# Index scores woven in portions into the left-over projections, and the first conv and attention spread over later ones

## The chip, the cores and the metric

The kernel runs on one core of a Trainium2 chip. Times are device microseconds of that core, medians over runs. Its engines are TensorE (PE; its weight loads are PEld), VectorE (DVE), ScalarE (ACT), GpSimd (POOL) and SyncE (SP), which here issues the transfers. Each engine takes its instructions in the order in which the compiled program holds them.

## The reference

A trunk of two layers over 2048 tokens of width 1024, in fp32. The even layer is an attention over 256 selected keys beside a causal depthwise convolution; the odd layer is a short convolution with gates.

```python
# even layer, u = rms_norm(x) @ w_in, split into q, k, v, qi, ki, wi, gate_a, glu_b, gate_b
dots  = einsum('bqhd,bsd->bqhs', qi, ki)                 # index scores, 8 heads of 64
score = einsum('bqh,bqhs->bqs', wi, relu(dots))
score = where(key <= query, score, -inf)
_, sel = top_k(score, 256)
a = softmax(q . k[sel] * 64**-0.5) . v[sel]              # 8 heads
a = a * silu(gate_a)
c = causal_depthwise_conv(g_lin * sigmoid(g_gate), cb_w) + cb_bias      # 31 taps
c = silu(layer_norm(c)) * silu(gate_b)
x = x + concat([a, c]) @ w_out
# odd layer, u = rms_norm(x) @ w_in, split into b_gate, c_gate, xin, gate
y = b_gate * causal_depthwise_conv(c_gate * xin, conv_w)                # 3 taps
x = x + (y * silu(gate)) @ w_out
out = rms_norm(x)
```

## The kernel before

The tokens are worked in 4 chunks of 512, each of 4 blocks of 128. Products of fp32 accuracy are made of three fp16 products (`mm3`, lines L189 to L191: high by high, high by low, low by high). `weight` (L195) loads a tile of weights; at its first use the tile is scaled on ScalarE (L210, L211), split on GpSimd (L212) and written back for later chunks (L213).

**Stage 1** makes everything of the even layer that all chunks need. For each chunk `project` computes keys, values, index queries and index keys. `index` (L720) computes a chunk's index scores: for each block, each stretch of up to 1024 keys and each head TensorE writes a tile `ps_i` (L737), ScalarE takes its Relu (L739), and VectorE adds it to the scores `sc` with the head's weight (L741). `select` (L752) then finds for two blocks at a time the 256th largest score of each row: it guesses a threshold, counts with two Sign passes on ScalarE (L792, `junk`), corrects it on VectorE (L796 to L807), and does so several times; then come the closing operations on VectorE, which count (L817), take the best 16 beyond the threshold (L822, L748 to L750), pick (L830, L831) and write a mask (L835); `bad` (L839) flags rows that were not settled. Chunk 0 has an exact selection instead (`general`, L276). `rest` holds what a chunk's projection leaves over: queries (`queries`, units "q") and the channels of the convolution and the gates (`channels`, units "g"), as a generator whose units the driver draws one by one.

Two more generators run in stage 1. `cn0` is the convolution of chunk 0: 120 multiply-adds of VectorE on the tile `cv` (L243), then its layer norm (L256 to L272) and four stores to `mc_dr`. `att` (`first_attention`, L860) is the attention of chunk 0, 32 heads in 4 blocks: logits on TensorE, mask and maximum on VectorE (L345), exponential (L352) and cast (L354) on ScalarE, a product on GpSimd (L355), a transpose through SP, values on TensorE (L372 to L374); at a block's end L396 to L404 on VectorE, and its store to `ma_dr` (L868).

**Stage 2** goes chunk by chunk. It begins at `mix(0)`: the loads `mh` and `ml` from `mc_dr` (L1141) and from `ma_dr` (L1143). `out_even` (L1013) multiplies the mix by the output weights `in_woe` in 8 tiles of 24 matmuls `ps_w<-mh/ml`, and VectorE adds the residual (L1023). The norm of these (L160 to L171, L1045) feeds the odd layer, whose first matmul is `ps_w<-xh`. Two units of gates, `ps_w<-xh` as well, stand around `out_even`; they store to `ga_dr` (L229). The attention of the later chunks and their convolution (tile `ps_c`, L243) run beside the odd layers.

What sets the order: a scheduler places each instruction by its place in the program and by priority; `weave(main, steps, (generator, rate), ...)` (L129) draws one unit of `main` after another and, with each, so many steps of the fillers as the rate says. While it draws fillers, `state["gate"]` is the last matmul of the main unit, and an instruction given to `paced` (L121) may not be placed ahead of it; this puts no wait on the chip.

Of the kernel before, what the change touches and what calls it, by code (L numbers as in the profile page):

```python
# [21 lines left out]
P = 128  # L22
# [21 lines left out]
NWT = 2  # L44
LOOK = 2
ALONE = 1
ATR = 3.5
CE, CX, CN0, CNR, R0, R1, R2 = 1.5, 3.0, 1.0, 0.85, 1.65, 1.65, 2.3
ORDER = ('ggqgqg', 'ggqgqg', 'gggg', 'qq')
EX = 1  # L50
TQ, TP = 2, 4
NA, NB1, KE, LG = 9, 7, 2, 1

SX = 2.0 ** 5
SW = 2.0 ** 8
# [19 lines left out]
def trunk_kernel(ctx: ExitStack, tc: tile.TileContext, xT, pos, wE, woE, wO, woO, par, tab, outT):  # L75
# [49 lines left out]
    def drain(gen):  # L125
        for _ in gen:
            pass

    def weave(main, steps=99, *fills):  # L129
        owed = [0.0] * len(fills)  # L130
        for n, _ in enumerate(main):
            state["gate"] = state["mm"]
            for i, (gen, rate) in enumerate(fills):
                owed[i] += rate
                while owed[i] >= 1.0:
                    owed[i] -= 1.0
                    next(gen, None)
            state["gate"] = None
            if n + 1 == steps:
                break  # L140
# [286 lines left out]
    with ExitStack() as es:  # L427
# [25 lines left out]
        def stats(c, held=None):  # L453
            eng = V if c <= STV else G
            acc = p0.tile([P, CH], FP32, name="ssum", bufs=1)
            for k in range(KD):
                x = held[k] if held else x_tile(c, k)
                square_into(p0, acc, x, k == 0, eng, (lambda: e1.tile([P, CH], FP32, name="th")) if c <= 1 else None)
            return acc
# [45 lines left out]
        def reload(c):  # L505
            xh = xp.tile([P, KD, CH], F16, name="xh")
            xl = xp.tile([P, KD, CH], F16, name="xl")
            for k in range(0, KD, 4):
                SP.dma_start(out=xh[:, k:k + 4, :], in_=xs_dr[c][:, 0, k:k + 4])
                SP.dma_start(out=xl[:, k:k + 4, :], in_=xs_dr[c][:, 1, k:k + 4])  # L510
            return xh, xl
# [206 lines left out]

        def index(c, qst, blocks):
            scs = {}  # L720
            first = cvp.tile([P, NJ, CH], FP32, name="cv") if c == 0 else None
            for i in blocks:
                b = c * TT + i
                W = (b + 1) * P
                if c == 0:
                    sc = first[:, i, 0:W]
                else:
                    sc = scp.tile([P, W], FP32, name=f"sc{i}", padded_shape=[P, (NB - TT + i + 1) * P])
                sm = tk.tile([P, 2], FP32, name=f"sm{i}")
                for sgi, s0 in enumerate(range(0, W, 1024)):  # L730
                    w = min(1024, W - s0)
                    for h in range(H):
                        ps = ps_i.tile([P, 1024], FP32, name="ps_i")
                        for r0 in range(0, w, 512):
                            r = min(512, w - r0)
                            for a in range(2):
                                T.matmul(out=ps[:, r0:r0 + r], lhsT=qst[:, h, i * P:(i + 1) * P], rhs=ki[:, a, s0 + r0:s0 + r0 + r], start=a == 0, stop=a == 1)  # L737
                        rl = e1.tile([P, 1024], FP32, name="relu")
                        A.activation(out=rl[:, 0:w], in_=ps[:, 0:w], func=AF.Relu)  # L739
                        kw = {"accum_out": sm[:, sgi:sgi + 1]} if h == H - 1 else {}  # L740
                        V.scalar_tensor_tensor(out=sc[:, s0:s0 + w], in0=rl[:, 0:w], scalar=wi[:, b, h:h + 1],  # L741
                                               in1=tiny[:, s0:s0 + w] if h == 0 else sc[:, s0:s0 + w],
                                               op0=ALU.mult, op1=ALU.add, **kw)
                scs[b] = (sc, sm, W)
            return scs

        def best16(out, x):
            V.max(out=out[:, 0:8], in_=x)  # L748
# [184 lines left out]
        def rest(c, xs):  # L933
            qs, ch = queries(c, xs), channels(c, xs)
            for unit in ORDER[c]:
                next(qs if unit == "q" else ch)
                yield
            yield from qs
            yield from ch

        def scan(c, xs):
            qst = project(c, xs)
            select(c, index(c, qst, (0, 1)))
            select(c, index(c, qst, (2, 3)))

        a, b, d = score_slot(3, 4), score_slot(0, 3), score_slot(1, 3)
        held = [a[:, k, :] for k in range(4)] + [b[:, k, :] for k in range(3)] + [d[:, 0, :]]
# [4 lines left out]
        qst = project(0, xs)  # L952
        x1 = first_normalize(1, acc, held)
        select_all(0, index(0, qst, (2, 3)))
        scan(1, x1)
        x2 = normalize(2, stats(2))
        r0 = rest(0, reload(0))
        weave(r0, NA)
        scan(2, x2)
        weave(r0)  # L960
        x3 = normalize(3, stats(3))
        r1 = rest(1, reload(1))

        def conv_out(j, x):
# [3 lines left out]

        cn0 = conv_norm(0, cvp, p0, ps_m, conv_out)
        att = first_attention()  # L970
        weave(r1, NB1, (cn0, CE), (att, ATR))
        scan(3, x3)
        weave(r1, 99, (cn0, CE), (att, ATR))
        state["scanned"] = True
        r2 = rest(2, reload(2))
        weave(r2, 99, (cn0, CE), (att, ATR))
        drain(cn0)
        held_last = reload(3)
        weave(rest(3, held_last), 99, (att, ATR))
        drain(att)  # L980


# [311 lines left out]
```

## Time and profile before

| | |
|---|---|
| median of 3 runs | 2196.25 us (2194.11 to 2197.8) |
| profiled execution | 2196.97 us, span 2195.2 us |
| granted TensorE clock, mean | 0.969 |
| TensorE busy | 1990.9 us (91%), 12252 matmuls |
| VectorE busy | 1663.6 us (76%) |
| ScalarE busy | 1174.1 us (53%) |
| GpSimd busy | 806.0 us (37%) |

Busy times are sums over a whole span with two unlike stages: stage 1 lasts to about 849 us, where the first output matmul starts, and the first odd matmul starts at 928.4 us. The clock is a share of full speed, of 2.4 GHz.

### The profile page before, as it was taken

The page shows a single profiled execution, that of the slowest core. Times are in us where ns is not written, and L with a number is a line of the kernel's source. Part 1 is how long each engine was busy: PE and PEld are TensorE (multiplying, and loading weights), DVE is VectorE, ACT ScalarE, POOL GpSimd, SP SyncE. Part 2 cuts the span into 40 slices and gives each one's busy share as a digit, 9 for nine tenths or more (in the row PEclk, how much of TensorE's full clock was granted, in tenths as well). Part 3 has the DMA queues.
Part 4 walks back from the last instruction along what each step waited for, and adds up shares of the span by engine and source line. Part 5 has one row for each costly group of instructions (what it writes and reads, how often), then busy time and mean ns, then how long its engine had stood idle before and what let it go on. Part 6 is the DMA issues. An engine that isn't in the chain of part 4 may idle for free. (4 is left out here: it accounts for less than half of the span.)

```text
span 2195.2 us, 34791 instructions
## 1 busy us (share of the span) xinstructions
PE 1990.9 (91%) x12252; PEld 1076.5 (49%) x12252; DVE 1663.6 (76%) x3485; ACT 1174.1 (53%) x2407; POOL 806.0 (37%) x761
## 2 busy tenths in 40 slices
PE   5777889898999999699999999999999999999997
PEld 3644464555464543244444454454544554444446
DVE  7999979998989884978875988873888887243224
ACT  5656656566477857367773645563555566121111
POOL 4765344535142412246762533441433454000000
PEclk9889999999999999899999999999999999999999
DMA  6445446334646476569875677785868798423234
GB/s 236 169 158 203 170 167 240 106 118 148 195 120 182 114 240 234 181 205 227 234 184 162 184 205 175 186 187 138 185 153 216 168 191 179 140 99 135 96 108 161
DMA packets 405475, 378.78 MB, mean 173 GB/s; under 512 B 313393, under 2 KB 333617, under 8 KB 384561
## 3 DMA queue, kind: packets, MB, share of 16 engines
q1 hardware_dynamic: 405296, 376.54, 60.5%
q8 instruction: 96, 1.57, 0.3%
q14 instruction: 83, 0.67, 0.1%
HBM read 214.35 MB, written 88.70 MB: 138 GB/s over the span
## 5 line engine op out<-in xcount | busy, mean ns | idle before, releaser
L355 POOL TENSOR_TENSOR pp<-lg,pp 128x512 f16<-128x512 f32 (+3 forms) x320 | 340.4, 1087 | 626.3 <-ACT pp L354 544.0
L189 PE MATMUL ps_w<-xh,wt 128*128 128x512 f16 (+1 forms) x1376 | 513.1, 374 | 7.9 <-DVE x L1023 4.2
L190 PE MATMUL ps_w<-xl,wt 128*128 128x512 f16 (+1 forms) x1376 | 513.7, 373 | 0.0
L191 PE MATMUL ps_w<-xh,wt 128*128 128x512 f16 (+1 forms) x1376 | 513.2, 373 | 0.0
L190 PEld LDWEIGHTS <-wt 128*128 128x128 f16 x2112 | 209.2, 99 | 247.4 <-issue 33.8
L189 PEld LDWEIGHTS <-wt 128*128 128x128 f16 x2112 | 209.7, 99 | 235.8 <-issue 17.7
L191 PEld LDWEIGHTS <-wt 128*128 128x128 f16 x2112 | 209.2, 99 | 234.8 <-issue 13.9
L243 DVE SCALAR_TENSOR_TENSOR ps_c<-cin,cwt,ps_c 128x512 f32<-128x512 f32 x348 | 261.2, 751 | 28.0 <-ACT ps_c L241 23.9
L352 ACT ACTIVATE lg<-lg,m 128x512 f32<-128x512 f32 (+3 forms) x320 | 207.0, 648 | 130.8 <-DVE m L345 130.4
L189 PE MATMUL ps_p<-xh,wt 128*128 128x512 f16 x480 | 186.4, 389 | 10.0 <-ACT th L224 5.5
L191 PE MATMUL ps_p<-xh,wt 128*128 128x512 f16 x480 | 185.1, 387 | 1.4 <-POOL wt L212 1.4
L190 PE MATMUL ps_p<-xl,wt 128*128 128x512 f16 x480 | 185.7, 387 | 0.0
L737 PE MATMUL ps_i<-ki,qst 128*128 128x512 f16 (+3 forms) x608 | 147.6, 360 | 31.0 <-ACT relu L739 29.5
L354 ACT CAST pp<-lg 128x512 f16<-128x512 f32 (+3 forms) x320 | 164.2, 547 | 21.1 <-DMA pt<-pp 17.4
L741 DVE SCALAR_TENSOR_TENSOR sc<-relu,wi,sc 128x1024 f32<-128x1024 f32 (+7 forms) x140 | 164.6, 1176 | 13.5 <-ACT relu L739 13.3
L739 ACT ACTIVATE relu<-ps_i 128x1024 f32<-128x1024 f32 (+7 forms) x176 | 142.1, 810 | 58.6 <-DVE sc L741 45.5
L189 PE MATMUL ps_p<-wt,xh 128*128 128x256 f16 (+1 forms) x608 | 167.2, 275 | 4.6 <-ACT u L596 2.5
L191 PE MATMUL ps_p<-wt,xl 128*128 128x256 f16 (+1 forms) x608 | 166.8, 276 | 0.8 <-DVE xl L491 0.8
L190 PE MATMUL ps_p<-wt,xh 128*128 128x256 f16 (+1 forms) x608 | 167.2, 275 | 0.0
L212 POOL TENSOR_TENSOR wt<-x,wt 128x512 f16<-128x512 f32 x80 | 98.6, 1264 | 149.2 <-ACT wt L211 124.8
L792 ACT ACTIVATE junk<-sc,t_x 128x640 bf16<-128x640 f32 (+5 forms) x84 | 118.7, 1413 | 58.0 <-DVE t_x L807 44.6
L1187 PE MATMUL ps_q<-kk,qs_a 128*128 128x512 f16 (+3 forms) x576 | 140.1, 353 | 9.4 <-DVE m L345 9.4
(288 smaller groups left out, 3544.1 us busy)
## 6 DMA issues: line engine op xcount, KB each, us to landing
wt<-w_in_wo_dram SPq DMA_DIRECT2D x48, 1024.0 KB, 5.1
wt<-w_in_we_dram SPq DMA_DIRECT2D x39, 1024.0 KB, 5.6
x<-in_wo_dram SPq DMA_DIRECT2D x64, 256.0 KB, 4.1
w_in_wo_dram<-wt SPq DMA_DIRECT2D x16, 1024.0 KB, 5.7
wt<-w_in_woo_dram SPq DMA_DIRECT2D x16, 1024.0 KB, 4.8
w_in_we_dram<-wt SPq DMA_DIRECT2D x13, 1024.0 KB, 4.9
w_stage<-in_we_dram SPq DMA_DIRECT2D x48, 256.0 KB, 3.1
wt<-w_in_woe_dram SPq DMA_DIRECT2D x12, 1024.0 KB, 4.9
```

What stands on the lines that cost most here:

```text
L189: T.matmul(out=out, lhsT=sh(k), rhs=mh(k), start=k == 0, stop=False)
L190: T.matmul(out=out, lhsT=sh(k), rhs=ml(k), start=False, stop=False)
L191: state["mm"] = T.matmul(out=out, lhsT=sl(k), rhs=mh(k), start=False, stop=k == KD - 1)
L243: ins = V.scalar_tensor_tensor(out=out if t == CK - 1 else acc, in0=ci[:, t:t + CH], scalar=cwt[:, j, t:t + 1], in1=acc, op0=ALU.mult, op1 ...
L352: A.activation(out=e, in_=e, func=AF.Exp, bias=last, scale=-1.0, accum_out=blk["ss"][:, h, si:si + 1])
L354: A.copy(out=pp[:, 0:w], in_=e)
L355: eng.tensor_tensor(out=pp[:, w:2 * w], in0=e, in1=pp[:, 0:w], op=ALU.subtract)
L737: T.matmul(out=ps[:, r0:r0 + r], lhsT=qst[:, h, i * P:(i + 1) * P], rhs=ki[:, a, s0 + r0:s0 + r0 + r], start=a == 0, stop=a == 1)
L739: A.activation(out=rl[:, 0:w], in_=ps[:, 0:w], func=AF.Relu)
L741: V.scalar_tensor_tensor(out=sc[:, s0:s0 + w], in0=rl[:, 0:w], scalar=wi[:, b, h:h + 1], in1=tiny[:, s0:s0 + w] if h == 0 else sc[:, s0:s0 ...
L792: A.activation(out=junk[:, 0:W], in_=sc, func=AF.Sign, bias=x[:, n:n + 1], scale=-1.0, accum_out=cn[:, n:n + 1])
L1187: ins = T.matmul(out=ps[:, 0:w], lhsT=qs[:, h, :], rhs=kk[:, a, s0:s0 + w], start=a == 0, stop=a == 1)
```

## The change

`index` becomes a generator, `score_blocks`, that stops after each portion (a tile of more than 512 keys, or two narrower ones), with `paced` on a portion's first matmul; `scan` becomes `selection`, which yields through the portions and then runs `select` for two blocks. The driver draws that generator, `find`, as a filler: chunk 1's in the first 5 units of chunk 0's rest, chunk 2's in its other units, chunk 3's in chunk 1's rest. The rates of `cn0` and `att` are 1.0 and 2.0 (1.5 and 3.5 before), and 0.4 of these in chunk 1's rest. Before, `cn0` and `att` began with the first 7 units of chunk 1's rest, ahead of chunk 3's scores, and chunk 0's rest (9 units) stood between chunk 1's and chunk 2's scores.

```diff
-ATR = 3.5
-CE, CX, CN0, CNR, R0, R1, R2 = 1.5, 3.0, 1.0, 0.85, 1.65, 1.65, 2.3
+ATR = 2.0
+CE, CX, CN0, CNR, R0, R1, R2 = 1.0, 3.0, 1.0, 0.85, 1.65, 1.65, 2.3
-NA, NB1, KE, LG = 9, 7, 2, 1
+NA, KE, LG = 5, 2, 1
+F1, F2, F3 = 6.5, 9.0, 6.0
...
         def index(c, qst, blocks):
             scs = {}
+            drain(score_blocks(c, qst, blocks, scs))
+            return scs
+
+        def score_blocks(c, qst, blocks, scs):
...
-                                T.matmul(out=ps[:, r0:r0 + r], lhsT=qst[:, h, i * P:(i + 1) * P], rhs=ki[:, a, s0 + r0:s0 + r0 + r], start=a == 0, stop=a == 1)
+                                ins = T.matmul(out=ps[:, r0:r0 + r], lhsT=qst[:, h, i * P:(i + 1) * P], rhs=ki[:, a, s0 + r0:s0 + r0 + r], start=a == 0, stop=a == 1)
+                                if r0 + a == 0:
+                                    paced(ins)
...
+                        if w > 512 or h % 2 == 1:
+                            yield
                 scs[b] = (sc, sm, W)
-            return scs
...
         def scan(c, xs):
             qst = project(c, xs)
-            select(c, index(c, qst, (0, 1)))
-            select(c, index(c, qst, (2, 3)))
+            return selection(c, qst)
+
+        def selection(c, qst):
+            for blocks in ((0, 1), (2, 3)):
+                scs = {}
+                yield from score_blocks(c, qst, blocks, scs)
+                gate, state["gate"] = state["gate"], None
+                select(c, scs)
+                state["gate"] = gate
...
-        scan(1, x1)
+        find = selection(1, project(1, x1))
+        r0 = rest(0, reload(0))
+        weave(r0, NA, (find, F1))
+        drain(find)
         x2 = normalize(2, stats(2))
-        r0 = rest(0, reload(0))
-        weave(r0, NA)
-        scan(2, x2)
-        weave(r0)
+        find = selection(2, project(2, x2))
+        weave(r0, 99, (find, F2))
+        drain(find)
         x3 = normalize(3, stats(3))
+        find = selection(3, project(3, x3))
         r1 = rest(1, reload(1))
...
-        weave(r1, NB1, (cn0, CE), (att, ATR))
-        scan(3, x3)
-        weave(r1, 99, (cn0, CE), (att, ATR))
+        weave(r1, 99, (find, F3), (cn0, 0.4 * CE), (att, 0.4 * ATR))
+        drain(find)
         state["scanned"] = True
-        r2 = rest(2, reload(2))
-        weave(r2, 99, (cn0, CE), (att, ATR))
+        weave(rest(2, reload(2)), 99, (cn0, CE), (att, ATR))
+        held_last = reload(3)
+        weave(rest(3, held_last), 99, (cn0, CE), (att, ATR))
         drain(cn0)
-        held_last = reload(3)
-        weave(rest(3, held_last), 99, (att, ATR))
         drain(att)
```

What the compiled programs hold at three places. On SP, at the seam of the two stages, before: the store of the last attention block (`ma_dr<-sq`), the load of chunk 0's mix behind it, and further down the first output weights (`in_woe`).

```order
L1141 DMA ml<-mc_dr 128x2048
L199 DMA wt<-w_in_we_dram_3273 128x4096
L868 DMA ma_dr<-sq 1024x1x128
L855 DMA cg_dr_132<-th 128x512
L836 DMA mb_dr_127<-mb 128x1792
L1143 DMA mh<-ma_dr 128x2048
L1143 DMA ml<-ma_dr 128x2048
L199 DMA wt<-w_in_we_dram_3352 128x4096
L855 DMA cg_dr_133<-th 128x512
L226 DMA gb_dr_138<-th 128x512
L199 DMA wt<-w_in_we_dram_3431 128x4096
L226 DMA gb_dr_138<-th 128x512 x3
L205 DMA x_9788<-in_woe_dram 128x512 x4
```

The same place of the changed program:

```order
L876 DMA ma_dr<-sq 1024x1x128
L1159 DMA mh<-ma_dr 128x2048
L1159 DMA ml<-ma_dr 128x2048
L230 DMA ga_dr_100<-th_9816 128x128
L230 DMA ga_dr_101<-th_9816 128x128
L230 DMA ga_dr_102<-th_9816 128x128
L230 DMA ga_dr_103<-th_9816 128x128
L230 DMA ga_dr_100<-th_9847 128x128
L230 DMA ga_dr_101<-th_9847 128x128
L230 DMA ga_dr_102<-th_9847 128x128
L230 DMA ga_dr_103<-th_9847 128x128
L206 DMA x_9788<-in_woe_dram 128x512 x4
```

The store, the mix, eight gate stores and the output weights now follow one another with nothing else between; before, channels (`cg_dr`, `gb_dr`) and two tiles of input weights (`w_in_we`) stood there.

On VectorE, around the first output tile (`x<-ps_w,xi`, L1023) before: the last search step of the last selection, its counting of both blocks, and the first closing operations between output tiles and the convolution of chunk 1 (`ps_c`).

```order
L805 TENSOR_TENSOR t_g<-t_g,t_gmin 128x2
L806 TENSOR_TENSOR t_g<-t_d,t_g 128x2
L807 TENSOR_TENSOR t_x<-t_x,t_g 128x2
L817 TENSOR_SCALAR mb,t_cn<-sc_7336,t_x 128x1920
L817 TENSOR_SCALAR mb,t_cn<-sc_7466,t_x 128x2048
L828 COPY t_cand<-t_x 128x2
L1023 SCALAR_TENSOR_TENSOR x_9786<-ps_w,xi 128x512
L822 SCALAR_TENSOR_TENSOR mk<-mb,sc_7336 128x1024
L243 SCALAR_TENSOR_TENSOR ps_c<-cin,cwt,ps_c 128x512
```

The changed program at its first output tile (L1039 there, L1023 before):

```order
L847 SCALAR_TENSOR_TENSOR bad<-t_j,t_Tn 128x2
L397 RECIPROCAL rc_9456<-ss_8766 128x8
L1172 TENSOR_REDUCE fl<-bad 128x1
L398 TENSOR_SCALAR rc_9456<-rc_9456 128x8
L186 TENSOR_TENSOR ssum<-cv,ssum 128x512
L273 SCALAR_TENSOR_TENSOR cv<-cv,cn_q 128x512
L399 TENSOR_TENSOR a_8818<-a_8818,rc_9456 128x512
L186 TENSOR_TENSOR ssum<-cv,ssum 128x512
L405 TENSOR_TENSOR x_in<-ps_m,x_in 128x512
L186 TENSOR_TENSOR sq<-x_in,sq 128x512
L244 SCALAR_TENSOR_TENSOR ps_c<-cin,cwt,ps_c 128x512
L1039 SCALAR_TENSOR_TENSOR x_9786<-ps_w,xi 128x512
```

The last selection's flag `bad` and the attention's last block (L397 to L405) now stand ahead of the first output tile; before, the attention had ended far ahead and the selection's closing operations stood behind it.

On TensorE, the rows ahead of the first output matmul (`ps_w<-mh`) before are a unit of gates:

```order
L189 LDWEIGHTS wt
L189 MATMUL ps_w<-xh,wt 128x512
L190 LDWEIGHTS wt
L190 MATMUL ps_w<-xl,wt 128x512
L191 LDWEIGHTS wt
L191 MATMUL ps_w<-xh,wt 128x512
L189 LDWEIGHTS wt
L189 MATMUL ps_w<-mh,wt 128x512
L190 LDWEIGHTS wt
L190 MATMUL ps_w<-ml,wt 128x512
```

In the changed program they are the values of the attention's last head (`vv`) and the turning of its last block (`id`):

```order
L375 MATMUL ps_m<-vv_5814,pt_9358 128x64
L373 LDWEIGHTS pt_9358
L373 MATMUL ps_m<-vv_5814,pt_9358 128x64
L374 LDWEIGHTS pt_9358
L374 MATMUL ps_m<-vv_5814,pt_9358 128x64
L375 LDWEIGHTS pt_9358
L375 MATMUL ps_m<-vv_5814,pt_9358 128x64
L403 MATMUL ps_m<-id_62,a_8818 128x128 x4
L190 LDWEIGHTS wt
L190 MATMUL ps_w<-mh,wt 128x512
L191 LDWEIGHTS wt
L191 MATMUL ps_w<-ml,wt 128x512
```

The gates' matmuls now stand ahead of the last 6 heads' values. Behind this place TensorE's order is the same in both programs.

## Rows read from the trace of the kernel before

**Rows 1.** windows; us, then busy us (instructions) of PE, PEld, DVE, ACT, POOL, clock, DMA
```profile
0.00:140.80 140.80, 90.50 (x738) 72.29 (x739) 123.50 (x254) 79.09 (x164) 91.54 (x99) 0.90 0.55 195
140.80:242.60 101.80, 86.16 (x515) 49.68 (x514) 100.69 (x243) 70.03 (x122) 48.22 (x41) 0.96 0.52 181
242.60:335.90 93.30, 82.17 (x527) 50.39 (x526) 74.40 (x248) 57.96 (x114) 41.83 (x50) 0.93 0.48 168
335.90:510.50 174.60, 152.97 (x1002) 91.31 (x1001) 172.54 (x310) 102.39 (x208) 77.86 (x75) 0.98 0.44 142
510.50:576.80 66.30, 61.90 (x376) 33.88 (x374) 60.17 (x149) 40.23 (x78) 20.98 (x26) 0.95 0.69 217
576.80:782.20 205.40, 191.71 (x1200) 108.12 (x1198) 180.47 (x390) 150.58 (x227) 73.39 (x68) 0.99 0.49 138
782.20:858.10 75.90, 69.70 (x322) 30.63 (x322) 37.68 (x133) 48.28 (x66) 6.21 (x6) 0.93 0.75 252
858.10:927.00 68.90, 51.79 (x226) 23.07 (x225) 65.98 (x111) 29.55 (x54) 24.72 (x20) 0.90 0.65 224
927.00:2195.20 1268.20, 1203.96 (x7358) 617.14 (x7357) 848.15 (x1660) 595.96 (x1382) 421.25 (x378) 0.98 0.66 170
```

**Rows 2.** waits of VectorE, 242.6 to 335.9 us: total, times, longest
```profile
DVE t_d L797 <- ACT junk L792: 15.4, 8, 3.7
```

**Rows 3.** waits of VectorE, 577 to 782 us
```profile
DVE sc L741 <- ACT relu L739: 15.6, 11, 3.7
DVE t_d L797 <- ACT junk L792: 6.2, 7, 2.7
```

**Rows 4.** waits of VectorE, 782 to 858 us
```profile
DVE t_d L797 <- ACT junk L792: 23.3, 6, 5.8
```

**Rows 5.** timeline of VectorE, a search step; start, duration, idle before and releaser
```profile
838.58 0.16 DVE L797 SCALAR_TENSOR_TENSOR t_d<-t_cn,t_wc 128x2 f32<-128x2 f32 x1 [4.04 <-ACT junk L792]
```

**Rows 6.** timeline of ScalarE, two Sign passes of the last selection
```profile
834.43 1.90 ACT L792 ACTIVATE junk<-sc,t_x 128x1920 bf16<-128x1920 f32 x1 [1.38 <-DVE t_x L807]
...
836.46 2.00 ACT L792 ACTIVATE junk<-sc,t_x 128x2048 bf16<-128x2048 f32 x1
```

**Rows 7.** timeline of VectorE, the first attention's last head and output
```profile
781.58 0.68 DVE L345 CUSTOM_DVE_ANT_0 lg<-ps_m,mb 128x512 f32<-128x512 f32 x1
...
804.90 0.69 DVE L404 TENSOR_TENSOR x_in<-ps_m,x_in 128x512 f32<-128x512 f32 x1
```

**Rows 8.** timeline of SP's queue around the mix of chunk 0
```profile
807.90 0.53 SPq L868 DMA_DIRECT2D ma_dr<-sq  x1
...
816.05 0.32 SPq L1143 DMA_DIRECT2D mh<-ma_dr  x1
...
841.32 1.76 SPq L205 DMA_DIRECT2D x<-in_woe_dram  x4
...
848.30 3.14 SPq L229 DMA_DIRECT2D ga_dr<-th  x4
```

**Rows 9.** windows of the seam between the stages, columns as in rows 1
```profile
849.40:858.10 8.70, 8.50 (x26) 2.99 (x27) 0.02 (x1) 8.70 (x14) 4.52 (x4) 0.64 0.95 328
858.10:896.50 38.40, 36.64 (x169) 16.39 (x168) 38.09 (x60) 18.66 (x35) 14.38 (x12) 1.00 0.73 252
896.50:913.00 16.50, 12.34 (x52) 5.35 (x50) 16.50 (x22) 6.11 (x11) 5.86 (x4) 0.90 0.52 173
913.00:928.40 15.40, 2.81 (x9) 1.33 (x10) 12.79 (x32) 5.79 (x10) 4.49 (x4) 0.64 0.52 187
```

**Rows 10.** one tile, cv on VectorE: duration ns min/median/max, first and last start
```profile
L243 DVE SCALAR_TENSOR_TENSOR cv<-cin,cwt,cv x120: 727/746/1696, 367.6 to 600.7; 128x512 f32<-128x512 f32 x120
```

**Rows 11.** waits of TensorE, 782.2 to 928.5 us
```profile
PE ps_m L171 <- DVE rs_d L165: 11.1, 1, 11.1
```

**Rows 12.** timeline of ScalarE around a table load
```profile
822.73 1.28 ACT L224 ACT_TABLE_LOAD   x1
824.02 0.60 ACT L224 ACTIVATE th<-ps_p 128x512 f32<-128x512 f32 x1
```

## The prediction

> **What bounds the kernel now.** I read the busy time of the engines by stretch first, with the stretches cut where VectorE takes the first and last index score of a chunk (L741), the first output tile of stage 2 (L1023) and the first normalized tile (L1045). From 927.0 us on TensorE is busy 1203.96 of 1268.20 us [rows 1], and the listing of the order shows the same TensorE order there in both kernels. So the question is when the first odd matmul starts (928.4 us, the end of the last window of [rows 9]); a shift of that moment passes one to one to the end.
>
> Ahead of it VectorE is nearly the bound. Its busy times from 0 to 927.0 add up to 815.4, so it idles 111.6 us: 17.3 before 140.8 us, 53.1 up to 782.2, 41.2 after that [rows 1]. In the middle, 335.9 to 510.5 us, it is busy 172.54 of 174.60. The waits name the idle time. While a selection searches its threshold, VectorE works ten tiny operations, then waits for two Sign passes of ScalarE over the scores (L792): 15.4 us in 242.6 to 335.9 [rows 2], 23.3 us in 782 to 858 [rows 4]. One round of the last selection with nothing between shows the price: 4.04 us idle [rows 5], behind Signs of 1.90 and 2.00 us [rows 6]. In 577 to 782 us the wait is for the Relu of the scores, 15.6 us [rows 3]: scores of chunk 3 come in bunches. Last, VectorE waits for the first output tile, busy 0.02 us in 849.4 to 858.1 [rows 9].
>
> **The change, part by part.** No operation is added or removed on TensorE, VectorE, GpSimd or the queues; ScalarE gets 12 table loads more. I priced each instruction of the changed order at the duration that its counterpart has in this trace and added up to each mark; the sums of before come out as [rows 1] has them. VectorE's work up to the mark, before and changed: first score of chunk 1 123.5 and 126.4; of chunk 2 298.6 and 283.2; of chunk 3 531.3 and 423.0; last score of chunk 3 711.8 and 635.7; first output tile 749.4 and 787.3; first normalized tile 815.4 and 818.5.
>
> So the scores run ahead and conv0 and the first attention fall behind. At chunk 3's first score only 2 of the 120 conv0 operations (L243, median 0.746 us [rows 10]) are done instead of 109, which is 84.9 us of the 108.3. Between the last score and the first output tile there are now 151.5 us of VectorE work instead of 37.7. The 113.8 more are 39 conv0 operations 30.5; 45 more closing operations of selections 37.5; 35 more search steps 11.4; 24 attention heads, where none stood, 11.6; conv0's norm 8.2; projections' and channels' operations 14.6. By the same pricing TensorE has 151 us there and ScalarE 127.5.
>
> *Idle time gained or lost.* I went through the 42 search rounds of the changed order and set the pair of Signs (4.0 us for the last blocks, less in proportion to the width before) against the VectorE work that stands between a step and the one that needs the Signs. What is not filled: chunk 1's rounds 4 us; chunk 2's 18, since there four rounds in a row have 0.0 to 0.2 us between and nothing of conv0 is left to put in; chunk 3's first half 1; its last half 16, where fills of 2.8, 0.6, 1.2, 2.4, 0.6 and 0 us stand in place of 0. That is 39 us against the 45 that the same wait cost in three stretches (15.4, 6.2 and 23.3 [rows 2 to 4]). The Relu wait, 15.6 us, has the portions to spread it; from nothing to all of it could stay, and I take 12. Idle time to the end of the last selection is then 17.3 + 39 + 12 = 68 us. The last head of the first attention starts at 780.1 us of VectorE work and the last selection's flag at 781.7: 848 and 850 us on the clock.
>
> *The tail.* That is where the bill comes. Before, the last head starts at 781.58 us, well ahead [rows 7], its block is stored at 807.90, the mix of chunk 0 is loaded behind that store at 816.05, and the first weights of the output projection are asked for at 841.32 [rows 8]: nothing waits for the attention. Now SP holds, in this order, the store, the load of the mix, eight gate stores and then the weights (the listing in the change's section). SP is in order, so the weights wait for the last head. From head to store the trace has 26.3 us, 23.3 of them up to the block's last operation (L404 at 804.90 [rows 7]), with conv0's norm and a selection in between on VectorE. In the changed order only 5.2 us of VectorE work lie between the two, and the matmuls of its last heads are all that TensorE has left; I take 16, bounds 10 and 26. Store to load 8.2 us with busy queues; I take 6, bounds 3 and 8.2. The load's two issues and eight gate stores, 3.14 us for four of these at the worst [rows 8], take 4. From the request for weights to the end of the first output tile the trace has 16.8 us (841.32 to 858.1), 8.7 of them at clock 0.64 [rows 8, 9]; kept. That gives 848 + 16 + 6 + 4 + 16.8 = 891. Seven more tiles took 38.4 us [rows 9]; 929. Then the norm: before, 896.5 to 928.4 is 32 us, because the closing operations of the last selection stand between its steps, and TensorE waits 11.1 us for L165 with the clock at 0.64 [rows 9, 11]. Those are now done earlier (all 36 of them, 31.4 us); 12.34 us of TensorE work remain in 896.5 to 913 [rows 9], of which some 8 lie ahead of the sum of squares, and the chain itself is some 6. I take 13. First odd matmul at 942 us, 13.6 later than 928.4.
>
> *Table loads.* One load is 1.28 us, and the next activation starts 0.01 us behind it [rows 12]. 12 more are 15.4 us of ScalarE, and 16 of the 31 now lie between the last score and the first output tile, inside the 127.5 above. ScalarE stays 18 us below VectorE's 146 there, so I add nothing; without that cover up to 15. The Trainium skill, "ScalarE: Activation LUTs", section "What ACT_TABLE_LOAD costs", gives 1.283 us for the load, as the trace does, and 1.38 us of drain besides, which the trace does not show. By its 2.66 us ScalarE would hold 149.6 us in the last stretch and the sum would be some 4 us higher; by the row nothing is added.
>
> **Sum.** The profiled execution took 2196.97 us, 0.7 above the median 2196.25. 2196.97 + 13.6 = 2210.6, less 0.7: **2210 us**.
>
> **Rivals.**
> *Faster: the weave fills the waits.* The idle time to the last head shrinks by more than the 14 us that the tail costs. VectorE in 335.9 to 510.5 us shows it can: 2.1 us idle in 174.6 with conv0 beside the scores [rows 1]. The 51 us of idle time behind chunk 1's first score would have to fall below 37; at 20 the last head is at 817, the first odd matmul at 911, the time 2179. Against it: conv0, the filler, now comes after chunk 2's search, whose rounds stand bare. Chance 0.30.
> *No change.* The tail is shorter by the 14 us: head to store in 10, the store's landing in 3, the staged weights at full clock (5.2 instead of 8.7 us for the first tile). 2196. Chance 0.16.
> *Slower still: the last stretch interlocks.* TensorE 151, VectorE 146 to the flag, ScalarE 127.5 depend on each other head by head. I gave it 166 us (0.88). In 242.6 to 335.9 us VectorE is busy 0.80 [rows 1]; at that it takes 182, 16 more: 2226. Chance 0.16.
> *ScalarE becomes the bound.* If each of the 16 loads in the last stretch cost once more what its row shows, 1.28 us, ScalarE had 148 us there, more than VectorE's 146, and at the same 0.88 the stretch would take 168: with the exchange between them some 4 us more, 2214. The gap of 0.01 us behind the load speaks against it [rows 12]. Chance 0.02. It is what the drain of the Trainium skill's "ScalarE: Activation LUTs" ("What ACT_TABLE_LOAD costs") would do here.
> My forecast, 2200 to 2218, has 0.36.
>
> **Numbers.** A measurement here tells about 0.2%, 4.4 us. Bounds: head to store -6 and +10, landing -3 and +2, Relu wait -12 and +4, bare rounds -15 and +6 (the 45 of before). To hold 8 in 10 the range goes from 2170, with nearly all of the faster cases, to 2230. Faster 0.30, same 0.16, slower 0.54 (0.36, 0.16 and 0.02).
>
> **What would show it.** Right: the first odd matmul near 942 us; SP issuing the load of the mix near 870 us and the first request for output weights right behind the gate stores; TensorE idle or at the low clock between about 864 and 890; chunk 3's first score near 461 us on VectorE and the last near 684 (before 576.8 and 782.2); Sign waits of some 18 us in chunk 2's search; the norm free of selection work. Wrong: the last head before about 834 us, which wipes out the loss, or a head-to-weights path of less than 13 us.

## The result, and the profile after

The changed kernel takes 2211.95 us (median of 5 runs, 2207.77 to 2216.42) against 2196.25: ratio 1.0074, 95% interval 1.0060 to 1.0089. It is slower by 15.7 us; the forecast was 2210, with a range of 2200 to 2218. The profiled execution took 2211.95 us, its span is 2210.2.

Stretches of the changed kernel, cut at the same events as [rows 1]: first score of chunks 1, 2 and 3, last score, the last selection's flag, first output matmul, first output tile, first odd matmul. Columns: us, busy time (instructions) of PE, PEld, DVE, ACT, POOL, granted clock of TensorE, DMA share, GB/s.

```profile
0.00:150.60 150.60, 106.86 (x823) 79.43 (x824) 132.06 (x279) 86.42 (x177) 95.12 (x103) 0.93 0.55 190
150.60:304.90 154.30, 125.13 (x828) 82.15 (x827) 150.77 (x402) 95.61 (x179) 78.23 (x81) 0.88 0.45 158
304.90:475.30 170.40, 153.05 (x922) 88.08 (x921) 145.74 (x344) 121.31 (x213) 59.91 (x64) 0.96 0.52 181
475.30:687.40 212.10, 195.53 (x1122) 105.77 (x1121) 198.34 (x400) 139.50 (x201) 55.18 (x57) 0.98 0.39 129
687.40:862.50 175.10, 148.18 (x929) 79.79 (x927) 143.17 (x350) 110.77 (x192) 53.20 (x54) 0.97 0.62 171
862.50:889.70 27.20, 2.76 (x28) 2.04 (x28) 4.26 (x8) 6.38 (x14) 1.15 (x1) 0.50 0.70 196
889.70:901.40 11.70, 11.63 (x41) 4.66 (x42) 0.81 (x2) 10.16 (x20) 9.04 (x8) 0.74 1.03 367
901.40:949.00 47.60, 45.23 (x212) 20.75 (x211) 30.68 (x54) 24.43 (x45) 16.94 (x14) 1.00 0.66 232
949.00:2210.20 1261.20, 1201.09 (x7358) 615.75 (x7357) 848.04 (x1658) 596.84 (x1384) 422.45 (x381) 0.98 0.66 172
```

The scores run ahead as forecast: chunk 3's first score stands at 475.3 us instead of 576.8 and its last at 687.4 instead of 782.2. VectorE's idle time in 150.6 to 304.9 us has fallen to 3.5 us (20.0 in the two windows of before). All that is given back: 24.7 us idle (8.2 before) in 304.9 to 475.3, 31.9 up to the flag, and then 27.2 us in which TensorE works 2.76 us and VectorE 4.26, with TensorE's clock at 0.50, its lower level. The first odd matmul starts at 949.0 us, 20.6 later than before; the rest takes 1254.5 us to the last matmul, 5.6 less than before.

How the seam runs in the changed kernel. VectorE: the last attention head, the last selection's flag, the last attention block's output, the first output tile.

```profile
860.72 0.68 DVE L346 CUSTOM_DVE_ANT_0 lg<-ps_i,mb 128x512 f32<-128x512 f32 x1
...
862.41 0.12 DVE L1172 TENSOR_REDUCE fl<-bad 128x1 f32<-128x16 f32 x1
...
870.54 0.69 DVE L405 TENSOR_TENSOR x_in<-ps_m,x_in 128x512 f32<-128x512 f32 x1 [0.61 <-PE ps_m L403]
...
901.35 0.69 DVE L1039 SCALAR_TENSOR_TENSOR x<-ps_w,xi 128x512 f32<-128x512 f32 x1 [0.67 <-PE ps_w L192]
```

SP's queue at the same place: the last store of the attention, the mix, the gate stores, the output weights.

```profile
873.29 0.52 SPq L876 DMA_DIRECT2D ma_dr<-sq  x1
879.08 0.32 SPq L1159 DMA_DIRECT2D mh<-ma_dr  x1
879.45 0.43 SPq L1159 DMA_DIRECT2D ml<-ma_dr  x1
881.05 3.79 SPq L230 DMA_DIRECT2D ga_dr<-th  x8
884.89 1.88 SPq L206 DMA_DIRECT2D x<-in_woe_dram  x4
```

ScalarE there: the cast of the stored block, then the table load of the gates' Silu, which waited 7.25 us, and the first scaling of the weights.

```profile
871.26 0.62 ACT L185 CAST sq<-x_in 128x512 f16<-128x512 f32 x1 [2.14 <-DVE x_in L405]
879.13 1.28 ACT L225 ACT_TABLE_LOAD   x1 [7.25 <-DMA ma_dr<-sq]
880.43 1.08 ACT L225 ACTIVATE th<-ps_w 128x512 f32<-128x512 f32 x2
...
888.43 0.63 ACT L211 ACTIVATE x<-x 128x512 f32<-128x512 f32 x1 [6.84 <-DMA x<-in_woe_dram]
```

And what TensorE waited for ahead of its first output matmul, 860 to 960 us (total, times, longest):

```profile
PE ps_w L190 <- ACT wt L212: 19.3, 1, 19.3
```

From the last head at 860.72 us everything hangs on one block: output at 870.54, store at 873.29, load behind the landed store at 879.08, gate stores at 881.05 because their Silu waited for the same store, weights asked for at 884.89, first output tile on VectorE at 901.35. Before, the same store left at 807.90, 50 us ahead of the first output tile [rows 8].

VectorE's waits in two stretches. 304.9 to 475.3 us, chunk 2:

```profile
DVE t_d L805 <- ACT junk L800: 12.1, 8, 2.8
DVE sc L748 <- ACT relu L746: 8.3, 8, 2.5
```

687.4 to 862.5 us, from the last score to the flag:

```profile
DVE t_d L805 <- ACT junk L800: 20.7, 8, 4.4
DVE lg L346 <- POOL pp L356: 5.7, 4, 2.8
```

### The profile page after: what moved, and what is told of

Same layout as the page of the kernel before. It is cut to its first block, busy times and chain, and to the rows that moved or that the text cites. A ratio compares the mean times of both kernels' runs of the same rounds, so it can differ in the third digit from the quotient of the medians.

```text
span 2210.2 us, 34826 instructions
## 1 busy us (share of the span) xinstructions
PE 1989.5 (90%) x12252; PEld 1078.4 (49%) x12252; DVE 1653.9 (75%) x3485; ACT 1191.4 (54%) x2419; POOL 791.2 (36%) x761
## 5 line engine op out<-in xcount | busy, mean ns | idle before, releaser
L355 ACT CAST pp<-lg 128x512 f16<-128x512 f32 (+3 forms) x320 | 164.1, 547 | 39.5 <-DMA pt<-pp 38.4
L379 PE MATMUL ps_v<-vv,pt 128*128 128x64 f16 (+1 forms) x2016 | 116.2, 207 | 28.0 <-DMA pt<-pp 27.1
```

Of the source, the lines that this page charges most:

```text
L355: A.copy(out=pp[:, 0:w], in_=e)
```

## The experiments

Each was timed in rounds beside the kernel before; the ratio is to the runs of the kernel before from those same rounds. The first odd matmul and VectorE's idle time are of the profiled executions; "chunk 1" is the idle time between the first scores of chunks 1 and 2, "chunk 2" that between the first scores of chunks 2 and 3, "rest" that from chunk 3's first score up to the first output tile. The column "rest" is to be compared with care: in before, e10 and e12 the last selection's flag comes behind that tile, in the others ahead of it.

| kernel | median us | ratio, 95% interval | first odd matmul | idle chunk 1 | chunk 2 | rest |
|---|---|---|---|---|---|---|
| before | 2196.25 | | 928.4 | 20.0 | 8.2 | 63.1 |
| changed | 2211.95 | 1.0074 (1.0060 to 1.0089) | 949.0 | 3.5 | 24.7 | 79.5 |
| e1_early_weights | 2215.07 | 1.0085 (1.0060 to 1.0111) | 950.7 | 3.6 | 24.4 | 79.8 |
| e2_old_rates | 2205.42 | 1.0051 (1.0035 to 1.0067) | 941.6 | 3.6 | 27.0 | 71.8 |
| e3_chunks12 | 2183.60 | 0.9957 (0.9941 to 0.9972) | 919.1 | 3.7 | 17.3 | 53.4 |
| e4_chunk3 | 2236.12 | 1.0187 (1.0158 to 1.0217) | 969.5 | 20.9 | 27.3 | 83.7 |
| e5_seam_first | 2221.08 | 1.0126 (1.0095 to 1.0158) | 957.1 | 3.6 | 26.8 | 84.4 |
| e6_late_weave3 | 2191.01 | 0.9983 (0.9968 to 0.9999) | 925.6 | 3.6 | 20.1 | 49.2 |
| e7_own_store | 2211.87 | 1.0079 (1.0050 to 1.0108) | 947.4 | 3.7 | 24.5 | 79.3 |
| e8_own_early | 2215.04 | 1.0097 (1.0065 to 1.0130) | 953.5 | 3.6 | 26.1 | 80.3 |
| e9_mix_not_late | 2200.68 | 1.0030 (1.0013 to 1.0046) | 938.6 | 3.6 | 26.0 | 69.1 |
| e10_chunk1 | 2200.82 | 1.0039 (1.0018 to 1.0059) | 935.0 | 19.5 | 11.2 | 65.2 |
| e11_chunk2 | 2190.49 | 0.9994 (0.9983 to 1.0005) | 924.2 | 5.4 | 16.9 | 58.0 |
| e12_five_units | 2187.59 | 0.9964 (0.9951 to 0.9978) | 924.8 | 6.5 | 18.5 | 54.9 |

Behind the first odd matmul all of them take 1253 to 1258 us to the last matmul (1260 before). So that moment tells nearly all of the difference between one variant and another; against before, 2 to 7 us come on top.

**e1_early_weights**

```diff
     weave(late, LG)
+    early = weight(wp, stg, woE, 0)
...
-    even = out_even(0, *m[0], x1, acc)
+    even = out_even(0, *m[0], x1, acc, early)
```

> The changed kernel with one edit: the first tile of output weights is asked for ahead of the loads of chunk 0's mix, so that on SP two of its four loads stand directly behind the last attention store and the other two ahead of the mix. In the changed kernel the weights were asked for at 884.9 us, 11.6 us behind that store (873.3), and the first output matmul waited 19.3 us for them. Theory (the queue makes the weights wait for the attention, and this staging is on the path): the first output matmul starts some 10 us earlier, at about 887 instead of 897 us, and the time falls by 8 to 12 us, to about 2202. Rival (the late mix itself is the bound, or the staging has to wait for memory that the first stage still holds): no more than 3 us.

The rival was right: 1.0085, no gain. (The first output matmul of the changed kernel starts at 889.76 us, not at 897 as the expectation has it; here it starts at 891.20.) SP's queue in this kernel:

```profile
872.68 0.52 SPq L876 DMA_DIRECT2D ma_dr<-sq  x1
873.25 1.67 SPq L206 DMA_DIRECT2D x<-in_woe_dram  x2
880.44 3.65 SPq L230 DMA_DIRECT2D ga_dr<-th  x8
884.13 0.90 SPq L206 DMA_DIRECT2D x<-in_woe_dram  x2
885.08 0.43 SPq L1160 DMA_DIRECT2D mh<-ma_dr  x1
```

Two of the four loads of weights left at once, but the other two and the mix now stand behind the gate stores, which still wait for the Silu (880.44). The load of the mix is issued at 885.08 instead of 879.08, and TensorE waits for that, 2 us longer than it had waited for the weights:

```profile
PE ps_w L190 <- DMA mh<-ma_dr: 21.3, 1, 21.3
```

So the weights were one of two strands of nearly the same length, not the only link.

**e2_old_rates**

```diff
-ATR = 2.0
-CE, CX, CN0, CNR, R0, R1, R2 = 1.0, 3.0, 1.0, 0.85, 1.65, 1.65, 2.3
+ATR = 3.5
+CE, CX, CN0, CNR, R0, R1, R2 = 1.5, 3.0, 1.0, 0.85, 1.65, 1.65, 2.3
```

> The changed kernel with the rates of before: conv0 1.5 and the first attention 3.5 instead of 1.0 and 2.0 (0.4 of these beside chunk 3's scores). Six fewer attention heads and 22 fewer conv0 operations stand behind the last score, and 79 VectorE rows lie between the last head and the first output tile instead of 14. Theory (the tail begins with the last store of attention or conv0): both end earlier, the time falls by some 5 to 10 us. Rival (idle time of VectorE in the search rounds decides): the last selection's rounds lose their filler, the idle time there grows by 5 to 10 us and the time stays or rises by as much.

The time falls by 6.5 us and the first odd matmul comes 7.4 us earlier, within the theory's 5 to 10, though the intervals of the two ratios still touch. The rival's rise of idle time did not come: 71.8 us in the last column against 79.5. The last attention store moves from 873.29 to 863.07 us, but conv0's last store comes only at 868.16 (869.96 in the changed kernel), so conv0 ends the first stage now.

**e3_chunks12**, the change for chunks 1 and 2 only:

```diff
-        weave(r1, 99, (find, F3), (cn0, 0.4 * CE), (att, 0.4 * ATR))
-        drain(find)
+        weave(r1, 7, (cn0, CE), (att, ATR))
+        drain(selection(3, project(3, x3)))
+        weave(r1, 99, (cn0, CE), (att, ATR))
...
-ATR = 2.0
+ATR = 3.5
```

> Half of the change: scores of chunks 1 and 2 woven, chunk 3's scan where it was before, with the rates of before and conv0 and attention begun ahead of it. Theory: attention and conv0 end early as in the kernel before, 109 us of VectorE work ahead of the first output tile for the last head, so the tail of the changed kernel is gone; the time is that of before or some us less, 2188 to 2198, as far as the weave fills waits. Rival (the weave of chunks 1 and 2 is what costs, by taking conv0 away from chunk 2's search): it stays near 2210.

Faster than both: 0.9957 (conv0's rate and the units of the later rests are those of before as well). The attention's store has its slack back, as SP's queue shows:

```profile
820.93 0.52 SPq L876 DMA_DIRECT2D ma_dr<-sq  x1
...
826.83 0.32 SPq L1160 DMA_DIRECT2D mh<-ma_dr  x1
...
853.52 1.76 SPq L206 DMA_DIRECT2D x<-in_woe_dram  x4
```

The store leaves 33 us ahead of the first request for output weights, the mix 27 us ahead.

**e4_chunk3**, the change for chunk 3 only:

```diff
-        find = selection(1, project(1, x1))
+        drain(selection(1, project(1, x1)))
+        x2 = normalize(2, stats(2))
         r0 = rest(0, reload(0))
-        weave(r0, NA, (find, F1))
+        weave(r0, 9)
...
-        weave(r0, 99, (find, F2))
-        drain(find)
+        drain(selection(2, project(2, x2)))
+        weave(r0)
```

> The other half: chunks 1 and 2 scanned in one piece as before, chunk 3's scores, conv0 and attention woven as in the change. 24 attention heads still stand behind the last score. Theory: the loss of the change is here, 2206 to 2216. Rival: 2194 to 2200.

The loss is here, and larger than either expected: 1.0187. It has the long tail of the changed kernel (last head at 878.29 us) and none of its gain ahead of chunk 2. Its two windows from the first score of chunk 1 to that of chunk 3:

```profile
141.20:336.10 194.90, 168.89 (x1040) 101.00 (x1039) 174.04 (x487) 127.93 (x234) 91.11 (x90) 0.94 0.51 175
336.10:496.20 160.10, 136.43 (x891) 85.90 (x890) 132.75 (x291) 98.66 (x178) 56.45 (x61) 0.93 0.42 146
```

20.9 us idle in the first, as before the change, and 27.3 in the second, where conv0 used to stand beside the search rounds.

**e5_seam_first**

```diff
+    early = weight(wp, stg, woE, 0)
+    for z in range(2):
+        SP.dma_start(out=mix(0)[z][:, 4:8, :], in_=mc_dr[:, z])
+    for z in range(2):
+        SP.dma_start(out=mix(0)[z][:, 0:4, :], in_=ma_dr[:, z])
     weave(late, LG)
-    for z in range(2):
-        SP.dma_start(out=mix(0)[z][:, 4:8, :], in_=mc_dr[:, z])
...
```

> The changed kernel with the output weights and the loads of chunk 0's mix both written ahead of the gate unit, so that on SP the eight gate stores stand behind both; the weights come right behind the mix load from the attention store. Asking for weights early alone had gained nothing: the mix load then moved behind the gate stores, and these wait for the gates' Silu, which itself starts only when the last attention store has landed (ScalarE idle 7.25 us for it in the changed kernel). Theory (the gate stores in SP's queue are the link between them): the first output tile ends some 5 to 9 us earlier than 901.3 us, the time falls to 2203 to 2207. Rival (the transfers themselves are the bound, whatever the order): within 3 us of the changed kernel.

Both were wrong: 9 us slower than the changed kernel. The mix (872.09) and the weights (873.23) do leave early, but the gate unit's own weights (`w_in_we`) now stand behind them (asked for at 880.53), and TensorE, which holds that unit ahead of the output matmuls, waits 22.5 us for them; its first output matmul starts at 900.8.

```profile
PE ps_w L190 <- DMA wt<-w_in_we_dram: 22.5, 1, 22.5
```

**e6_late_weave3**, e3 with chunk 3's scores woven behind the start of conv0 and attention:

```diff
-        drain(selection(3, project(3, x3)))
-        weave(r1, 99, (cn0, CE), (att, ATR))
+        find = selection(3, project(3, x3))
+        weave(r1, 99, (find, 20.0), (cn0, CE), (att, ATR))
+        drain(find)
```

> Chunks 1 and 2 woven, conv0 and attention begun as before the change, and chunk 3's scores woven into the last units of chunk 1's rest behind that. Theory (what costs is the attention pushed behind chunk 3's scores, not the weaving of these): about the 2183.6 us of the half change, 2178 to 2190. Rival (weaving chunk 3's scores costs by itself, by bare search rounds): 2195 or more.

2191.01 lies just beyond the theory's range and short of the rival's: most of the changed kernel's loss is gone with the attention early (first odd matmul 925.6 instead of 949.0), and weaving chunk 3 still costs 6.5 us of that moment against e3.

**e7_own_store**

```diff
-                hl = p0.tile([P, 2, 4, P], F16, name="sq", bufs=1)
+                hl = e1.tile([P, 2, 4, P], F16, name="relu", padded_shape=[P, 4, 4, P]) if b == TT - 1 else p0.tile([P, 2, 4, P], F16, name="sq", bufs=1)
```

> The changed kernel with the last attention block stored from the memory of a Relu tile instead of from sq, whose place the gates' tile of stage 2 takes over. Theory (the Silu waits for that memory): ScalarE's wait of 7.25 us ahead of the gates' Silu is gone and the gate stores are issued at once behind the load of the mix; the weights are asked for some 1 to 2 us earlier, since the load of the mix still waits for the store; the time falls by 0 to 3 us. Rival (the gates wait for something else): the Silu still starts near 879 us.

The mechanism shows, the time does not move (1.0079). ScalarE:

```profile
869.22 0.62 ACT L185 CAST relu<-x_in 128x512 f16<-128x512 f32 x1 [2.14 <-DVE x_in L405]
869.85 1.28 ACT L225 ACT_TABLE_LOAD   x1
...
886.88 0.63 ACT L211 ACTIVATE x<-x 128x512 f32<-128x512 f32 x1 [14.57 <-DMA x<-in_woe_dram]
```

The Silu's table load follows the cast at once, 9 us earlier than in the changed kernel; the wait was for the memory under the stored block. But the load of the mix still waits for the store (877.17 us), the gate stores and weights stand behind it, and the first request for weights moves only from 884.89 to 883.20.

**e8_own_early**, e1 and e7 together.

> Both: the early request for weights and the last attention block stored from another memory. Theory (the two were linked by the gate stores): now the gate stores leave ahead of the landing, the weights are asked for near 873 to 878 us, the load of the mix is issued near 880 instead of 885, and the first output matmul starts near 885; the time falls by 4 to 9 us against the changed kernel, to 2203 to 2208. Rival: as with the early request alone, no gain.

No gain either: 1.0097. SP's queue:

```profile
876.36 0.52 SPq L876 DMA_DIRECT2D ma_dr<-relu  x1
882.35 0.81 SPq L206 DMA_DIRECT2D x<-in_woe_dram  x2
883.26 3.82 SPq L230 DMA_DIRECT2D ga_dr<-th  x8
...
888.07 0.43 SPq L1160 DMA_DIRECT2D mh<-ma_dr  x1
```

Now the weights' staging waits for the memory of the stored block, as the Silu did before; SP's waits at this place (total, times, longest) have it:

```profile
SPq L206 <- DMA ma_dr<-relu: 5.4, 1, 5.4
```

The load of the mix comes behind all that at 888.07, and TensorE waits 20.3 us for it.

**e9_mix_not_late**

```diff
     for z in range(2):
-        SP.dma_start(out=mix(0)[z][:, 4:8, :], in_=mc_dr[:, z])
+        for k in (4, 6):
+            SP.dma_start(out=mix(0)[z][:, k:k + 2, :], in_=mc_dr[:, z, 0:2, :])
     for z in range(2):
-        SP.dma_start(out=mix(0)[z][:, 0:4, :], in_=ma_dr[:, z])
+        for lo in (0, 2 * P):
+            SP.dma_start(out=mix(0)[z][:, 0:4, lo:lo + 2 * P], in_=ma_dr[:, z, :, 0:2 * P])
```

> The changed kernel in which chunk 0's mix is loaded without the late parts: blocks 0 and 1 of the attention stand in for 2 and 3 and channel tiles 0 and 1 of conv0 for 2 and 3. The same work is done and the same bytes are loaded, but the first output matmul waits neither for the last attention store nor for the last two conv stores. Theory (the first output tile waits for the late attention, by way of its store, the load of the mix and what stands behind them on SP): the first output matmul starts 8 to 14 us earlier than 889.8, and the time falls to 2198 to 2204. Rival (all of stage 1's work is late, and the seam would take as long without that dependence): within 3 us of the changed kernel, 2209 to 2215.

The theory: 2200.68 us, ratio 1.0030 instead of 1.0074. The mix leaves out the late blocks, so this kernel does not compute the reference; the amount of work is the same. The first output matmul starts 11.5 us earlier (889.76 in the changed kernel); it waits for the first weights, as it does there, but 10.33 us instead of 19.3:

```profile
878.21 0.61 PE L190 MATMUL ps_w<-mh,wt 128*128 128x512 f16 x1 [10.33 <-ACT wt L212]
```

SP's queue shows where the time goes:

```profile
870.01 0.52 SPq L876 DMA_DIRECT2D ma_dr<-sq  x1
872.50 0.51 SPq L985 DMA_DIRECT2D mc_dr<-ssum  x1
873.06 1.09 SPq L206 DMA_DIRECT2D x<-in_woe_dram  x2
```

From the last attention store to the first request for weights it is 3.05 us instead of 11.6: 8.5 us are the landing, the load of the mix and the gate stores. Another 3.3 us are not the missing dependence itself: the compiled order has shifted with it, the last head stands at 850.43 us instead of 860.72 and the store leaves that much earlier. And one link is still there: the weights stand behind the two last stores in SP's queue. So the experiment shows the links behind the store to be worth some 8.5 to 11.5 us, not the whole loss; of the 20.6 us at the first odd matmul 10.2 remain.

**e10_chunk1** and **e11_chunk2**, e3 (the "half change" of the expectations) with the weave of one chunk only:

```diff
-        find = selection(2, project(2, x2))
-        weave(r0, 99, (find, F2))
-        drain(find)
+        weave(r0, 4)
+        drain(selection(2, project(2, x2)))
+        weave(r0)
```

> Only chunk 1's scores are woven, into the first 5 units of chunk 0's rest; chunks 2 and 3 as before the change. In the changed kernel VectorE's idle time between the first scores of chunks 1 and 2 is 3.5 us against 20.0 before, and between the first scores of chunks 2 and 3 24.7 against 8.2. Theory (each weave trades one chunk's idle rounds for another's filler; chunk 1's gains, chunk 2's loses): idle time up to chunk 2's first score about 4 us, and 2 to 8 behind it, the time 2176 to 2186, below the half change's 2183.6 or at it. Rival (the gain of the half change comes from chunk 2's weave): 2190 to 2198.

```diff
-        find = selection(1, project(1, x1))
-        r0 = rest(0, reload(0))
-        weave(r0, NA, (find, F1))
-        drain(find)
+        drain(selection(1, project(1, x1)))
         x2 = normalize(2, stats(2))
+        r0 = rest(0, reload(0))
+        weave(r0, NA)
```

> Only chunk 2's scores are woven, into the last 5 units of chunk 0's rest; chunk 1 and chunk 3 as before the change. Theory: VectorE keeps the 20 us of idle time up to chunk 2's first score and gets some 17 to 25 us in chunk 2's stretch, since conv0 is not there to fill its search rounds: 2198 to 2208. Rival (weaving chunk 2 gains): 2180 to 2192.

My theory fell in both, and in e10 the rival's range as well (2200.82 us). Chunk 1 woven alone is slower than before (1.0039), chunk 2 alone takes as long (0.9994). The idle time between the first scores of chunks 1 and 2 does not follow the weave: 19.5 us with chunk 1 woven, 5.4 with it not woven. It follows the number of units of chunk 0's rest ahead of chunk 2's scores: 9 in e10, e4 and before, 5 in the others.

**e12_five_units**, the kernel before with that number alone:

```diff
-NA, NB1, KE, LG = 9, 7, 2, 1
+NA, NB1, KE, LG = 5, 7, 2, 1
```

> The kernel before with one number changed: 5 instead of 9 units of chunk 0's rest ahead of chunk 2's scan, nothing woven. What the runs so far leave open is whether the half change gains by weaving or by bringing chunk 2's scores ahead of four units. Theory (the place of the four units is the gain: every kernel in which chunk 2's first score comes behind 5 units has 4 to 5 us of VectorE idle time before it, and both with 9 units have 20): chunk 2's first score near 312 us instead of 335.9, idle time ahead of it about 5 us, the time 2180 to 2190. Rival (the weaving is the gain): idle time as before, 2193 to 2200.

The theory: 0.9964 (0.9951 to 0.9978), not to be told from e3's 0.9957. Its windows from the first score of chunk 1 to that of chunk 2 and on to that of chunk 3:

```profile
142.70:307.30 164.60, 140.51 (x927) 88.95 (x926) 158.10 (x418) 101.33 (x190) 83.91 (x84) 0.95 0.43 150
307.30:562.10 254.80, 218.54 (x1329) 123.71 (x1327) 236.26 (x501) 159.81 (x308) 96.26 (x103) 0.93 0.51 164
```

6.5 us idle in 164.6 us where before had 20.0 in 195.1. Behind it, though, 18.5 us are idle where before had 8.2, so most of that is lost again. The gain inside the change is the four units moved; weaving chunks 1 and 2 together adds nothing that can be measured. One at a time it costs: e11 differs from e12 only by the weave of chunk 2 and loses the gain (0.9994, the intervals do not meet), and e10 differs from before by the weave of chunk 1 and is 0.4% slower. Why the two together come out even is open. So is a part of e12's gain: its first odd matmul is 3.6 us earlier than before, the other 5 us lie behind it, where before takes 1260.1 us and e12 1254.8.

## Why the prediction was right

*The seam sets the end.* Right in the mechanism: the last head comes late, store, mix, gate stores and weights follow one another on SP, and the first odd matmul moves. That the number came out within 2 us was luck in part. The first odd matmul was forecast at 942 us, 13.6 later than before, and came at 949.0, 20.6 later; the profiled time grew by only 15, because the second stage took 5.6 us less, which the forecast had not expected ("one to one"). Three misses make this up: the last head 12.7 us later than forecast, the tail behind it 5.7 us shorter, the second stage 5.6 us shorter. Why the second stage is shorter is open; in the other kernels it takes 1253.2 to 1258.4 us against 1260.1, each in one execution, so a part of it may be the spread between executions.

*VectorE's clock times.* First score of chunk 1: forecast 143.7 from the sum (126.4 + 17.3), measured 150.6; VectorE worked 132.1 us there and idled 18.5. One unit of the rest more stands ahead of it (75 of its matmuls on TensorE instead of 2); all kernels with chunk 1 woven have it near 151, the others near 142. Chunk 2: 307 and 304.9. Chunk 3: 461 and 475.3. Last score: 684 and 687.4. Last head: 848 and 860.7. Up to the flag the work was 770.1 us, not 781.7, and the idle time 92.4, not 68: two errors of opposite sign that left the 12.7 us. Why the same operations took 11.6 us less than at the durations of before is open.

*The search rounds.* The count of unfilled rounds gave 39 us; the waits have 37.1. The parts agree less than the sum: 2.3, 12.1, 2.0 and 20.7 us in the four stretches from chunk 1's first score to the flag, where 4, 18, 1 and 16 were forecast; the 18 us in chunk 2's search, one of the signs of being right, did not show. The Relu wait was 17.4 us against 12. The other 19 us of idle time were not in the sum: 5.7 of them are the attention's own chain (VectorE for GpSimd's product).

*The tail.* Forecast 94 us from the last head to the first odd matmul, measured 88.3; with the forecast in brackets, head to store 12.6 (16), store to mix 5.8 (6), mix to weights 5.8 (4), weights to first tile 16.5 (16.8), seven tiles 33.0 (38.4), norm 14.6 (13). SP issued the load of the mix at 879.08 us, 9 later than the sign of being right had it, since the last head came late. The tail's cause was only half told: I had the weights waiting in SP's queue behind the attention's load. e1, e7 and e8 show two more links of about the same length, the load of the mix itself and the memory that the stored block holds, so undoing the queue alone gains nothing; e9, which frees the mix from the late parts, gains 10.4 us at the first odd matmul (some 3 of them by a shifted order), and e3, in which conv0 and attention are early, 30.

*The rivals.* The idle time ahead of chunk 2's first score did fall by 16.5 us (e12 shows that the four moved units do 13.5 of that without any weave), and as much was lost behind it, 16.5, where the argument against the faster case had put it: conv0 is missing as a filler. No run tests that alone, but the kernels line up with it. Where conv0's first operation comes 32 or 35 us behind chunk 2's first score (before, e10), that stretch has 8.2 and 11.2 us idle; at 80 to 94 us (e3, e6, e11, e12) 16.9 to 20.1; from 114 us on (all others) 24.4 to 27.3. The last stretch ran at 0.82 (143.17 of 175.1), nearer to the interlock's 0.80 than to my 0.88, with 3 us less work: there the rival for a still slower kernel was the nearer one (175 us; it had 182, I had 166), and the shorter tail and second stage hid it. Table loads: 31 in all, each 1.283 us:

```profile
L225 ACT ACT_TABLE_LOAD x14 | 18.0, 1283 | 7.5 <-DMA ma_dr<-sq 7.3
L353 ACT ACT_TABLE_LOAD x14 | 18.0, 1283 | 0.3
```

ScalarE's timeline around one of them in the changed kernel, between an exponential and a Silu:

```profile
705.53 0.19 ACT L353 ACTIVATION_READ_ACCUMULATOR lg<-lg,m 128x1 f32 x1
705.74 1.28 ACT L225 ACT_TABLE_LOAD   x1
707.03 0.60 ACT L225 ACTIVATE th<-ps_p 128x512 f32<-128x512 f32 x1
```

0.02 us ahead and 0.01 behind. Of the 28 loads above, the idle time ahead is 0.5 us in all beside the one wait for the store. The drain of 1.38 us that the Trainium skill, "ScalarE: Activation LUTs" ("What ACT_TABLE_LOAD costs"), adds is not in these rows; the measurement decides for this kernel, and ScalarE, busy 110.77 of the last stretch's 175.10 us, was not the bound that this rival made of it.

## What to carry to other kernels

When work is moved ahead to fill an engine, look at what it moves behind: here conv0 and the attention were the filler of one chunk's waits and the input of the next stage, and pushed to the end they turned 50 us of slack into a wait. Undoing one link of such a chain gained nothing while another of the same length stood beside it; freeing the late input showed what the links behind it are worth. And a change of several parts should be taken apart before it is judged: the whole lost 15.7 us, and one of its numbers alone, 5 units instead of 9, gained 8.

## What the runs showed that I had not expected

In this kernel a store held its memory until it landed, and that memory was the place of the next stage's tile: ScalarE stood 7.25 us ahead of a Silu for a DMA with which the Silu has nothing else in common, and when the store was moved to other memory (e7) that wait went away, to come back at the weights' staging tile (e8, 5.4 us).
